# Three moves in the mixer of a hybrid block: which engine takes four w_ada tiles, where the expert bias rows are loaded, where silu(c) is computed

## Chip, cores and metric

The kernel runs on one core of a Trainium2 chip. The metric is the device time of one execution in microseconds (us); the median of several runs counts. Engine names as in the profile: PE is TensorE, DVE is VectorE, ACT is ScalarE, POOL is GpSimd, SP is SyncE, whose queue issues most loads from HBM.

## The reference, cut to what matters

One sequence of 256 tokens of width 1024, one conditioning vector `c`, all in float32.

```python
ada = (silu(c) @ w_ada + b_ada)                      # 6 x 1024 values
sh1, sc1, g1, sh2, sc2, g2 = split(ada, 6)
h = rmsnorm(x) * (1 + sc1) + sh1
xr, gr, q, k, v, gate_r, gate_a = split(h @ w_in + b_in)
y_rnn = rg_lru(conv(xr)) * gelu(gr)                  # RG-LRU: a scan over the tokens
y_att = sliding_window_attention(q, k, v, sinks)
merged = sigmoid(gate_r) * (y_rnn @ w_o_rnn) + sigmoid(gate_a) * (y_att @ w_o_attn)
x = x + g1 * rmsnorm(merged @ w_out)
h = rmsnorm(x) * (1 + sc2) + sh2
x = x + g2 * rmsnorm(moe(h))                         # top 4 of 32 experts: w1, b1, SwiGLU, w2, b2
```

The adaLN values `ada` are a matrix-vector product with 24 MB of w_ada. Only sh1 and sc1 are needed at the start; the rest is needed after the mixer.

## The kernel before, in words

**Memory.** All large weights come through one ring of 18 slots of 8 KB per partition (`ring`, L57), tag "w"; a load into a slot waits until the slot's last reader is done. The split parts hi and lo of a weight, and some intermediates, take slots of the same ring. Small intermediates of 2 KB per partition rotate through five buffers (`t2`, L72). PSUM is split into three banks with tag "p" and five with tag "a" (`bank`, L75). The order of the instructions on each engine is the program's order; nothing reorders them (L62).

**Start (L79 to L181).** SP loads c, x and the first w_ada and w_g1 tiles. ACT and DVE compute silu(c) spread over all partitions (`sc_`, L120, L121), then silu(c) as a column per chunk (`scc`: Sigmoid L124, product L125) and a column `one_each` (a reduction, L127); the last two are used only by the tiles of w_ada that PE takes. Then come the squares of x (ACT L131, DVE L132), the Sqrt and reciprocal (L158, L159), the normed rows `xn` (L161, L162) and their transposes. ACT has to load a function table before some functions; these loads are instructions of their own in the profile.

**The chunk loop (L234 to L274).** For each of the eight chunks k of the input width: DVE takes two dots with w_ada (L137), which give sh1 and sc1 of the chunk, two short operations make the factors `am` (L245, L247), ACT makes hT and its rounded part hTh (L253, L254), `split` (L184) makes the rounded part hi of the weights on ACT (L190) and the rest lo on DVE (L193), DVE makes hTl (L230). PE multiplies the chunk before into all eight banks (L267, then three passes of L273: hi with hTh, hi with hTl, lo with hTh).

**The mixer, steps 0 to 21 (L547, L620).** Step i issues loads (`ISSUE`, L35), splits the weights of step i+1 (ACT L190, DVE L193), runs the evacuation of step i-1 (`late_work`), and multiplies its own pair of weight tiles into a "p" bank (`mm_pair`, L285, matmuls at L295; step 5 is the v projection, `mm_v`, whose evacuation is DVE's L319). Steps 0 to 13 read h, 14 to 17 the attention's output `ya`, 18 to 21 the scan's output `yr`. Between these, `run` (L579) does the small tasks that `PLAN` (L34) names by letter, one list in the middle of a step and one after it: attention (M, X, E, N, T, P), convolution, gates and scans (s, c, m, R, g, h, d, D, q, S, y) and the later w_ada tiles (A). T is the transposes of the attention's products (PE L504), which need the products of N (DVE L492). y3, after step 17, makes the last quarter of yr (ACT L430, DVE L431).

**The later w_ada tiles.** Sixteen tiles remain, taken in the order of the letter A; index 4 and 5 stand after step 5 ("X02 E00 D0 A M10 A"), 9 after step 12, 10 after step 13, 11 in the middle of step 15. A tile whose index is in `ON_PE` (L37) goes to PE; the others are two dots on DVE (`ada_dot`, L136, L137). On PE a tile is eight matmuls into a "p" bank (`ada_mm`, L140, L145) with a copy by ACT (L148), and, at the next call of `run`, two matmuls and a copy (`ada_sum`, L151 to L155); the bank is held until then. How a tile is laid out in HBM follows `ON_PE`, on the host.

**After step 21 (L631 to L880).** ACT issues six loads, two halves of b2 (`b2s`, L649, 64 KB each) and four pieces of b1 (`b1t`, L654, 128 KB each, two `t2` buffers). DVE does some short operations (L631 to L662). ACT copies b1t into the rounded `b1r` (L664, twice), DVE takes the rest (L665, twice). Then steps 22 to 25 split the w_o tiles, evacuate the last step (`merge_r`, L607: DVE L612 and L613, ACT L614, DVE L615), and PE multiplies by w_out (L202) and spreads column vectors over the partitions (`spread`, L637, PE L643, ACT L644). Router and experts follow; SP loads the expert weights w1 and w2 (383 tiles of 1 MB) through the ring. The first of them are issued from step 21 on (letter e in `ISSUE`). SP and ACT put their loads on separate queues, but a load can also be made to wait for the landing of an earlier one, of either queue.

Of the kernel before, what the change touches and what calls it, by code (L numbers as in the profile page):

```python
# [8 lines left out]
F32 = mybir.dt.float32  # L9
F32R = mybir.dt.float32r  # L10
I32 = mybir.dt.int32
AF = mybir.ActivationFunctionType
OP = mybir.AluOpType
AX = mybir.AxisListType
ENG = mybir.EngineType

P = 128
# [4 lines left out]
E = 32  # L22
# [11 lines left out]
PLAN = {0: ('', 'g0 s1'), 1: ('', 'h0 c1 s0 c0'), 2: ('A', 'g1 m1 A'), 3: ('R1 A M00 m0', 'h1 A R0 X00'), 4: ('d1 M01', 's3 X01'), 5: ('d0 M02', 'X02 E00 D0 A M10 A'), 6: ('', 'M11 N00 X10 M12'), 7: ('E01 s2 X11 N01', 'X12 T000 A'), 8: ('P00 T010', 'E10 c2 A T011'), 9: ('P01 m2', 'N10 c3 E11'), 10: ('', 'N11 D1 g3 q0 q1 S0 T100'), 11: ('P10 A T110', 'R2 T111 g2 m3'), 12: ('R3 P11', 'h2 A'), 13: ('S1', 'h3 d2 D2 d3 D3 A'), 14: ('', 'q2 S2 q3 y0 S3'), 15: ('A y2', ''), 16: ('y1', 'A'), 17: ('', 'A y3'), 19: ('', 'A A')}  # L34
ISSUE = {-1: 'wwaww', 0: 'aw', 2: 'w', 5: 'a', 8: 'aw', 11: 'w', 14: 'aa', 19: 'aw', 21: 'w', 22: 'aw', 28: 'w', 29: 'w', 31: 'w', 33: 'a', 36: 'aa', 37: 'aw', 42: 'w', 43: 'wawwa', 49: 'w', 50: 'w', 52: 'awa', 54: 'w', 60: 'w', 64: 'e', 69: 'ww', 71: 'e', 72: 'e', 74: 'e', 76: 'eee'}  # L35
BIG = 3.0e38
ON_PE = (2, 4, 5, 7, 9, 11)  # L37

VEC = {}
_o = 0  # L40
# [11 lines left out]
def tile_hybrid_block(ctx: ExitStack, tc: tile.TileContext, x_in, c, vecs, rows, w_ada, w_g1, w_qk, w_v, w_gate,  # L52
                      w_bd, w_or, w_oa, w_o, w_router, w1, b1, w2, b2, out):
    nc = tc.nc
    consts = ctx.enter_context(tc.tile_pool(name="consts", bufs=1))
# [16 lines left out]
    def t2(shape=(512,), parts=P, name="t2"):  # L72
        return tmp.tile([parts] + list(shape), F32, name=name, tag="t2")
# [17 lines left out]
    def v(name, j=None):  # L91
        o, w = VEC[name]
        return vec[:, o:o + w] if j is None else vec[:, o + j:o + j + 1]
# [7 lines left out]
    b = bank("p")  # L101
# [19 lines left out]
    nc.vector.tensor_tensor(sc_, cb, sc_, op=OP.mult)  # L121
    nc.scalar.activation(warm, eps, AF.Sqrt)
    scc = consts.tile([P, KC], F32, name="scc")
    nc.scalar.activation(scc, v("c"), AF.Sigmoid)  # L124
    nc.vector.tensor_tensor(scc, v("c"), scc, op=OP.mult)  # L125
    one_each = consts.tile([P, 1], F32, name="one_each")
    nc.vector.tensor_reduce(one_each, ident.rearrange("p (a b) -> p a b", a=4)[:, :, 0], axis=AX.X, op=OP.add)  # L127
    lt = consts.tile([P, 4, 8], F32, name="lt")
    ada = consts.tile([P, 48], F32, name="ada")
    junk = rtile((2, D), "junk")  # L130
# [45 lines left out]
    o_, _ = VEC["b_ada"]  # L176
# [57 lines left out]
    for k in range(KC + 1):  # L234
# [6 lines left out]
        if k < KC:  # L241
            wt = rtile((2048,), "w")
            for h in range(2):
                nc.sync.dma_start(out=wt[:, h * D:(h + 1) * D], in_=w_g1[k, :, h * D:(h + 1) * D])
            nc.vector.scalar_tensor_tensor(am[:, 0, k:k + 1], ada[:, 8 + k:9 + k], scb[:, k:k + 1], v("n_pre_mix", k),  # L245
                                           op0=OP.add, op1=OP.mult)
            nc.vector.tensor_tensor(am[:, 1, k:k + 1], ada[:, k:k + 1], vec[:, o_ + k:o_ + k + 1], op=OP.add)  # L247
            if k == 1:
                lru_scales()
            hT[k] = t2((S,), name="hT")  # L250

            def make_h(k=k):
                nc.scalar.activation(hT[k], xnT[:, k], AF.Identity, scale=am[:, 0, k:k + 1], bias=am[:, 1, k:k + 1])  # L253
                nc.scalar.activation(hTh[:, k], hT[k], AF.Copy)  # L254

            if k < PLAIN:
                make_h()
                whl[k] = wt
            else:
                whl[k] = split(wt, make_h)  # L260
                low_h(k)
# [358 lines left out]
    for i in range(22):  # L620
        if i == 14:
            mg = big.tile([P, KC, S], F32, name="mg", tag="h")
        mid, after = PLAN.get(i, ("", ""))
        step(i, evac[i], lambda: run(mid))
        if i == 0:
            for f in range(8):
                b_ = g1b[4 + f // 2][:, (f % 2) * S:(f % 2 + 1) * S]
                nc.scalar.activation(gr[:, f], b_, AF.Identity, bias=v("b_gr", f))
        run(after)
# [14 lines left out]
            nc.scalar.activation(dst(i), b, AF.Copy)  # L644

    rws = big.tile([P, 2, D], F32, name="rws", tag="h")
    b2s = [big.tile([E, 512], F32, name="b2s", tag=tag) for tag in ("k", "v")]
    for i in range(2):
        nc.scalar.dma_start(out=b2s[i], in_=b2[:, i * 512:(i + 1) * 512])  # L649

    b1t, b1r = [t2() for _ in range(2)], consts.tile([P, 2, 512], F32R, name="b1r")
    for h in range(2):
        for i in range(2):
            nc.scalar.dma_start(out=b1t[h][64 * i:64 * i + 64], in_=b1[64 * h:64 * h + 64])  # L654
    sel = consts.tile([P, 64], F32R, name="sel")
    nc.vector.tensor_tensor(sel, ident[:, 0:64], ident[:, 64:128], op=OP.add)
    sel2 = consts.tile([64, E], F32R, name="sel2")
# [737 lines left out]
```

## Time and profile before

| | |
|---|---|
| median of 3 runs | 1255.26 us (1253.52 to 1258.53) |
| the profiled execution | 1256.51 us |
| its span, first to last instruction | 1254.9 us |
| mean granted PE clock | 0.969 |
| PE busy | 1156.5 us, 92% of the span |
| DVE busy | 479.5 us, 38% |
| ACT busy | 279.5 us, 22% |
| moved from HBM | 466.61 MB, 373 GB/s over the span |

Times in the rows are those of the profiled execution, from the start of its span. Busy shares are averages over stages with different limits: the mixer ends near 250 us, the router near 300, and the experts take the rest. What a part of the kernel is worth is read from the stage that it lies in. Granted clock 1.00 is 2.4 GHz, 0.50 is 1.2 GHz.

### The profile page before, as it was taken

The page shows a single profiled execution, that of the slowest core. Times are in us where ns is not written, and L with a number is a line of the kernel's source. Part 1 is how long each engine was busy: PE and PEld are TensorE (multiplying, and loading weights), DVE is VectorE, ACT ScalarE, POOL GpSimd, SP SyncE. Part 2 cuts the span into 40 slices and gives each one's busy share as a digit, 9 for nine tenths or more (in the row PEclk, how much of TensorE's full clock was granted, in tenths as well). Part 3 has the DMA queues.
Part 4 walks back from the last instruction along what each step waited for, and adds up shares of the span by engine and source line. Part 5 has one row for each costly group of instructions (what it writes and reads, how often), then busy time and mean ns, then how long its engine had stood idle before and what let it go on. Part 6 is the DMA issues. An engine that isn't in the chain of part 4 may idle for free. (4 is left out here: it accounts for less than half of the span.)

```text
span 1254.9 us, 15487 instructions
## 1 busy us (share of the span) xinstructions
PE 1156.5 (92%) x6003; PEld 558.9 (45%) x6003; DVE 479.5 (38%) x918; ACT 279.5 (22%) x523; POOL 10.4 (1%) x23
## 2 busy tenths in 40 slices
PE   7997999969899999999999999999979999998886
PEld 5995979946233333333343333333323333332322
DVE  6877787934522323222313223222223232222222
ACT  6466597233211101000101010000101110000002
POOL 0000000000100000000000000000000000000000
PEclk8998999979899999999999999999989999999999
DMA  9964456597889999999999999999999999999995
GB/s 366 405 248 168 168 202 272 232 343 294 363 334 422 421 421 421 421 421 421 421 420 421 422 394 420 421 421 421 421 418 420 420 421 420 421 421 421 421 420 213
DMA packets 68176, 468.74 MB, mean 374 GB/s; under 512 B 7616, under 2 KB 8000, under 8 KB 13696
## 3 DMA queue, kind: packets, MB, share of 16 engines
q1 hardware_dynamic: 67392, 466.67, 90.8%
q10 hardware_dynamic: 704, 1.02, 0.3%
q8 instruction: 48, 0.79, 0.3%
q14 instruction: 32, 0.26, 0.1%
HBM read 466.61 MB, written 1.05 MB: 373 GB/s over the span
## 5 line engine op out<-in xcount | busy, mean ns | idle before, releaser
L1008 PE MATMUL bank_a<-w,xg 128*64 128x512 f32 x2048 | 471.3, 605 | 11.4 <-PEq L1170 6.6
L1008 PEld LDWEIGHTS bank_a<-w,xg 128*64 128x64 f32 x2048 | 139.9, 139 | 293.6 <-issue 261.6
L1041 PE MATMUL bank_a<-w,aT 128*64 128x512 f32 x960 | 216.8, 600 | 9.1 <-ACT aT L1035 7.4
L1089 DVE TENSOR_SCALAR G<-bank_p,slot 128x256 fp32r<-128x256 f32 x32 | 15.5, 484 | 409.9 <-PE bank_p L1084 409.9
L1035 ACT ACTIVATE aT<-bank_p 128x512 f32<-128x512 f32 x31 | 18.5, 597 | 525.1 <-PE bank_p L1031 525.1
L1041 PEld LDWEIGHTS bank_a<-w,aT 128*64 128x64 f32 x960 | 66.1, 137 | 141.8 <-issue 115.7
L1062 DVE TENSOR_TENSOR ff<-ff,bank_p 128x512 f32<-128x512 f32 x124 | 79.7, 684 | 65.4 <-PE bank_p L1059 65.4
L193 DVE TENSOR_TENSOR lo<-w,hi 128x1024 fp32r<-128x1024 f32 x66 | 78.3, 1220 | 26.9 <-ACT hi L190 26.9
L1049 DVE SCALAR_TENSOR_TENSOR ys<-bank_a,gslot,ys 128x512 fp32r<-128x512 f32 x31 | 23.3, 751 | 146.6 <-ACT ys L1048 146.6
L190 ACT ACTIVATE hi<-w 128x1024 fp32r<-128x1024 f32 x66 | 66.1, 1052 | 6.1 <-DVE lo L193 4.2
L1059 PE MATMUL bank_p<-ys,G 64*128 64x512 f32 x248 | 49.2, 469 | 14.3 <-DVE ys L1049 13.5
L1048 ACT ACTIVATE ys<-bank_a,gslot 128x512 fp32r<-128x512 f32 x31 | 21.3, 688 | 167.6 <-PE bank_a L1041 164.0
L822 PE MATMUL bank_p<-pm,hth 128*128 128x256 f32 x112 | 33.3, 326 | 13.5 <-DVE pm L804 13.5
L137 DVE SCALAR_TENSOR_TENSOR w<-w,cs 128x1024 f32<-128x1024 f32 x36 | 42.5, 1220 | 0.0
L1059 PEld LDWEIGHTS bank_p<-ys,G 64*128 64x128 f32 x248 | 20.1, 196 | 47.5 <-issue 24.7
L295 PE MATMUL bank_p<-hTh,hi 128*128 128x256 f32 x208 | 31.5, 295 | 9.3 <-DVE vv L319 9.3
L822 PEld LDWEIGHTS bank_p<-pm,hth 128*128 128x128 f32 x112 | 22.6, 202 | 35.8 <-issue 18.3
L1004 PE MATMUL bank_a<-b1r,pick 128*128 128x512 f32 x124 | 37.7, 423 | 0.0
L1021 ACT ACTIVATE ys<-gl 128x512 f32<-128x512 f32 x33 | 20.8, 630 | 73.5 <-DVE gl L1020 73.5
L1004 PEld LDWEIGHTS bank_a<-b1r,pick 128*128 128x128 f32 x124 | 20.7, 188 | 29.4 <-issue 26.8
L295 PEld LDWEIGHTS bank_p<-hTh,hi 128*128 128x128 f32 x208 | 27.3, 195 | 13.2 <-DVE vv L319 9.8
L1020 DVE TENSOR_SCALAR gl<-bank_a 128x512 f32<-128x512 f32 x33 | 22.7, 686 | 22.3 <-PE bank_a L1008 16.9
(347 smaller groups left out, 1151.1 us busy)
## 6 DMA issues: line engine op xcount, KB each, us to landing
w<-in_w_dram SPq DMA_DIRECT2D x383, 1024.0 KB, 19.8
w<-in_w_ada_dram SPq DMA_DIRECT2D x16, 1024.0 KB, 6.5
w<-in_w_ada_dram SPq DMA_DIRECT2D x16, 512.0 KB, 10.2
w<-in_w_g_dram SPq DMA_DIRECT2D x16, 512.0 KB, 9.9
w<-in_w_gate_dram SPq DMA_DIRECT2D x8, 1024.0 KB, 5.3
w<-in_w_qk_dram SPq DMA_DIRECT2D x5, 1024.0 KB, 9.4
w<-in_w_oa_dram SPq DMA_DIRECT2D x4, 1024.0 KB, 6.3
w<-in_w_or_dram SPq DMA_DIRECT2D x4, 1024.0 KB, 8.2
```

Of the source, the lines that this page charges most:

```text
L137: nc.vector.scalar_tensor_tensor(wt[:, n], wt[:, n], 1.0, sc_, op0=OP.mult, op1=OP.mult, accum_out=ada[:, j:j + 1])
L190: nc.scalar.activation(hi[:, c_], w[:, c_], AF.Copy)
L193: nc.vector.tensor_tensor(lo[:, c_], w[:, c_], hi[:, c_], op=OP.subtract)
L295: nc.tensor.matmul(b[:, n], w[n][m][:, k * P:(k + 1) * P], z[l][:, k], start=k == 0 and i == 0 and (n == 0 or not late), stop=k == KC - 1 ...
L822: nc.tensor.matmul(ps[:, n], z[:, t, f * P:(f + 1) * P], pms[:, t].rearrange("p a b -> p (a b)"), start=t == 0 and n == 0 if len(ts) == 1 ...
L1004: nc.tensor.matmul(o, m.rearrange("p a b -> p (a b)"), z, start=False, stop=False)
L1008: nc.tensor.matmul(o[q * CAP:(q + 1) * CAP], xk(k), w1t[k][:, c0:c0 + 512], start=k == 0, stop=k == KC - 1)
L1020: nc.vector.tensor_scalar(gl, bb[0], LIMIT, None, op0=OP.min)
L1041: nc.tensor.matmul(y[q * CAP:(q + 1) * CAP], aT[:, k % 4, k // 4 * CAP:(k // 4 + 1) * CAP], w2t[k // 2][:, k % 2, q * 512:(q + 1) * 512], ...
L1049: nc.vector.scalar_tensor_tensor(lo, y, G[1], hi, op0=OP.mult, op1=OP.subtract)
L1059: nc.tensor.matmul(b[q], G[0][qs, t * P:(t + 1) * P], ys[i][qs], start=i == 1, stop=i == 0)
L1062: nc.vector.tensor_tensor(d, d, b[q], op=OP.add)
```

## The change

There are three edits. The list `ON_PE` has four indices instead of six: 4, 9 and 11 go from PE to DVE, and 10 goes from DVE to PE, so that no two of the listed ones are neighbours in the order. The six loads of b2 and b1 are issued inside the loop over the steps, by ACT, after step 17 and ahead of the tasks that follow it (a w_ada tile and y3), instead of after step 21; their readers stay where they were. The column silu(c) for PE and `one_each` are computed in the third chunk of the chunk loop (k = 2), after the two short operations for `am`, instead of at the start.

```diff
--- before.py
+++ after.py
@@ -34,7 +34,7 @@
 BIG = 3.0e38
-ON_PE = (2, 4, 5, 7, 9, 11)
+ON_PE = (2, 5, 7, 10)
 
 VEC = {}
 _o = 0
@@ -121,10 +121,7 @@
     nc.vector.tensor_tensor(sc_, cb, sc_, op=OP.mult)
     nc.scalar.activation(warm, eps, AF.Sqrt)
     scc = consts.tile([P, KC], F32, name="scc")
-    nc.scalar.activation(scc, v("c"), AF.Sigmoid)
-    nc.vector.tensor_tensor(scc, v("c"), scc, op=OP.mult)
     one_each = consts.tile([P, 1], F32, name="one_each")
-    nc.vector.tensor_reduce(one_each, ident.rearrange("p (a b) -> p a b", a=4)[:, :, 0], axis=AX.X, op=OP.add)
     lt = consts.tile([P, 4, 8], F32, name="lt")
     ada = consts.tile([P, 48], F32, name="ada")
     junk = rtile((2, D), "junk")
@@ -247,6 +244,10 @@
             nc.vector.tensor_tensor(am[:, 1, k:k + 1], ada[:, k:k + 1], vec[:, o_ + k:o_ + k + 1], op=OP.add)
             if k == 1:
                 lru_scales()
+            if k == 2:
+                nc.scalar.activation(scc, v("c"), AF.Sigmoid)
+                nc.vector.tensor_tensor(scc, v("c"), scc, op=OP.mult)
+                nc.vector.tensor_reduce(one_each, ident.rearrange("p (a b) -> p a b", a=4)[:, :, 0], axis=AX.X, op=OP.add)
             hT[k] = t2((S,), name="hT")
 
             def make_h(k=k):
@@ -622,6 +623,15 @@
             mg = big.tile([P, KC, S], F32, name="mg", tag="h")
         mid, after = PLAN.get(i, ("", ""))
         step(i, evac[i], lambda: run(mid))
+        if i == 17:
+            b2s = [big.tile([E, 512], F32, name="b2s", tag=tag) for tag in ("k", "v")]
+            for h in range(2):
+                nc.scalar.dma_start(out=b2s[h], in_=b2[:, h * 512:(h + 1) * 512])
+
+            b1t, b1r = [t2() for _ in range(2)], consts.tile([P, 2, 512], F32R, name="b1r")
+            for h in range(2):
+                for n in range(2):
+                    nc.scalar.dma_start(out=b1t[h][64 * n:64 * n + 64], in_=b1[64 * h:64 * h + 64])
         if i == 0:
             for f in range(8):
                 b_ = g1b[4 + f // 2][:, (f % 2) * S:(f % 2 + 1) * S]
@@ -644,14 +654,6 @@
             nc.scalar.activation(dst(i), b, AF.Copy)
 
     rws = big.tile([P, 2, D], F32, name="rws", tag="h")
-    b2s = [big.tile([E, 512], F32, name="b2s", tag=tag) for tag in ("k", "v")]
-    for i in range(2):
-        nc.scalar.dma_start(out=b2s[i], in_=b2[:, i * 512:(i + 1) * 512])
-
-    b1t, b1r = [t2() for _ in range(2)], consts.tile([P, 2, 512], F32R, name="b1r")
-    for h in range(2):
-        for i in range(2):
-            nc.scalar.dma_start(out=b1t[h][64 * i:64 * i + 64], in_=b1[64 * h:64 * h + 64])
     sel = consts.tile([P, 64], F32R, name="sel")
     nc.vector.tensor_tensor(sel, ident[:, 0:64], ident[:, 64:128], op=OP.add)
     sel2 = consts.tile([64, E], F32R, name="sel2")
```

## Rows read from the trace of the kernel before

**Rows 1.** The chain that ended last (page), shares of the span by engine.

```profile
DMA 22%; PE 3%; DVE 1%; issue 0%; ACT 0%; DVEq 0%; SPq 0%
```

**Rows 2.** By stage: length, busy PE PEld DVE ACT POOL, PEclk, DMA, GB/s.

```profile
142.00:180.00 38.00, 37.74 (x295) 31.14 (x293) 30.53 (x54) 30.90 (x71) 0.00 (x0) 1.00 0.48 177
213.60:247.60 34.00, 33.62 (x279) 33.30 (x278) 32.28 (x44) 12.58 (x15) 0.47 (x4) 1.00 0.73 290
122.38:140.77 18.39, 15.37 (x112) 14.77 (x113) 15.51 (x32) 8.48 (x25) 0.00 (x0) 0.81 0.31 115
260.00:270.00 10.00, 3.03 (x9) 2.56 (x10) 5.38 (x9) 4.03 (x6) 0.00 (x0) 0.50 1.02 409
400.00:1218.00 818.00, 770.42 (x3533) 279.42 (x3531) 215.93 (x398) 77.98 (x140) 0.00 (x0) 0.98 1.01 420
```

**Rows 3.** Timeline, start and last chunk: start, duration, engine, line, operation, tiles, [idle].

```profile
8.10 1.28 ACT L124 ACT_TABLE_LOAD   x1
11.10 1.28 ACT L158 ACT_TABLE_LOAD   x1 [0.45 <-DVE junk L132]
12.39 0.29 ACT L158 ACTIVATE rs<-small 128x2 f32<-128x2 f32 x1
9.79 1.22 DVE L132 SCALAR_TENSOR_TENSOR junk<-x 128x1024 f32<-128x1024 f32 x1
62.11 0.42 DVE L230 TENSOR_TENSOR hTl<-hT,hTh 128x256 fp32r<-128x256 f32 x1
64.96 0.88 PE L273 MATMUL bank_p<-hTl,hi 128*128 128x256 f32 x6
```

**Rows 4.** Timeline, TensorE at step 6, VectorE and TensorE at the transposes.

```profile
125.40 2.08 PE L295 MATMUL bank_p<-hTh,hi 128*128 128x256 f32 x8 [9.31 <-DVE vv L319]
138.87 1.90 DVE L492 TENSOR_TENSOR att<-att,den 128x512 f32<-128x512 f32 x3
141.73 1.03 PE L504 MATMUL bank_a<-ident,att 128*128 128x128 f32 x8
```

**Rows 5.** Timeline, one w_ada tile on each engine: L145 and one of two L137.

```profile
190.78 1.07 PE L145 MATMUL bank_p<-w,scc 128*32 128x256 f32 x16
202.86 1.22 DVE L137 SCALAR_TENSOR_TENSOR w<-w,cs 128x1024 f32<-128x1024 f32 x1
```

**Rows 6.** Waits of SP, 190 to 380 us; timeline, 250 to 276 us.

```profile
SPq L66 <- DMA b2s<-in_b_dram: 12.8, 1, 12.8
SPq L66 <- DMA t<-in_b_dram: 8.3, 4, 3.2
...
250.06 0.63 ACT L614 ACTIVATE mgp<-mg 128x512 fp32r<-128x512 f32 x1 [2.80 <-DVE mg L613]
250.92 2.46 ACTq L654 DMA_DIRECT2D t<-in_b_dram  x4
262.35 0.63 ACT L664 ACTIVATE b1r<-t 128x512 fp32r<-128x512 f32 x1 [5.20 <-DMA t<-in_b_dram]
...
252.21 0.16 DVE L662 TENSOR_TENSOR slot<-slot 128x1 f32<-128x1 f32 x1
...
251.84 0.62 PE L202 MATMUL bank_a<-hi,mgp 128*128 128x512 f32 x2
266.97 1.11 PE L643 MATMUL bank_p<-ident,ada 128*128 128x128 f32 x4 [11.22 <-DVE t L612]
267.74 0.77 PE L202 MATMUL bank_a<-hi,mgp 128*128 128x512 f32 x1
275.41 0.39 PE L202 MATMUL bank_a<-hi,mgp 128*128 128x512 f32 x1
```

**Rows 7.** Load issued 213.6 to 214.2 us; timeline of steps 17, 18.

```profile
w<-in_w_ada_dram SPq DMA_DIRECT2D x1, 1024.0 KB, 7.8
...
225.21 2.01 ACT L190 ACTIVATE hi<-w 128x1024 fp32r<-128x1024 f32 x2 [4.20 <-DVE lo L193]
...
227.98 0.69 DVE L431 TENSOR_TENSOR yr<-gr,yr 128x512 fp32r<-128x512 f32 x1
```

## Prediction, made before the change was run

> **What bounds the kernel now.** Read the chain that ended last first [rows 1]: 22% of the span is transfers of expert weights and everything else together is some 5%, so the end is set by a stream of loads. The table by stage confirms it [rows 2]: from 400 to 1218 us the DMA share is 1.01 at 420 GB/s, and the change touches nothing there. A transfer-bound tail moves only as a whole, by as much as the work ahead of it hands over sooner; that work ends before 400 us, and each microsecond saved in it counts once. So each part is priced in its own stage. In the same table, from 142 to 180 us TensorE is busy 37.74 of 38 us; from 213.6 to 247.6 us TensorE is busy 33.62 and VectorE 32.28 of 34 us, both nearly full; from 260 to 270 us TensorE works 3.03 of 10 us at a granted clock of 0.50. That last hole is the dearest, and the waits around it lead straight to one part of the change [rows 6].
>
> **silu(c) moved.** The program starts with a table load for L124's Sigmoid at 8.10 us and one for L158's Sqrt at 11.10 us, 1.28 us each; behind the second, L158 runs at 12.39 [rows 3]. The Sigmoid stands between two Sqrt, so without it both loads go. The DVE square L132, held to 9.79 us by the two silu operations ahead of it, can start at about 8.1, when ScalarE's first load would have begun: 1.69 sooner. With the load of 1.28 that is 2.97 us, which TensorE inherits through xn. Will it keep them? In the chunk loop VectorE is as busy as TensorE: its last hTl is ready at 62.11 + 0.42 = 62.53 us, and TensorE's pass over it starts at 64.96 [rows 3]. If VectorE gained nothing and the two moved short operations cost it 0.3 us (0.16 us each, as L662 [rows 6]), TensorE could still move by 64.96 − 62.85 = 2.1 us. Bounds 2.1 and 3.0; VectorE's first dots start earlier too, so I take **2.8**. The Sigmoid's load in the third chunk falls where ScalarE waits for VectorE: nothing there. The Trainium skill (ScalarE: Activation LUTs, What ACT_TABLE_LOAD costs) charges a drain of some 1.4 us beside a load of 1.28. By that the two loads would give 2.8 us more, 5.6; the row, whose Sqrt starts at 12.39 = 11.10 + 1.28 + 0.01, shows no drain behind the load, so the sum goes without it.
>
> **The tile of step 5 (index 4).** Today two tiles in a row after step 5 run on TensorE, and each holds one of three p banks; the third holds the v projection. Step 6 then waits 9.31 us, until 125.40, for the DVE evacuation of v (L319) [rows 4]. With index 4 on VectorE a bank is free, and step 6 can start some 9 us sooner. That is not the gain: the transposes L504 at 141.73 need att_norm's products (L492), which end at 138.87 + 1.90 = 140.77, and VectorE has to do two more dots of 1.22 us ahead of them [rows 4, 5]. From 122.38 to 140.77 VectorE is busy 15.51 of 18.39 us [rows 2]: 2.9 us of waits, on ScalarE and TensorE work that now comes sooner. If all go, L492 ends at 140.77 + 2.44 − 2.9 = 140.3 and TensorE gains 1.4 us; if none go, it loses 140.77 + 2.44 − 141.73 = 1.5. Most of the waits are for engines that gain, so I take **1.0**. From 142 us TensorE is the bound and carries it on.
>
> **Indices 9, 10 and 11.** Two tiles go from TensorE to VectorE and one comes back. TensorE is relieved of one tile net, 1.07 us of L145; VectorE gets one net, 2 × 1.22 = 2.44 [rows 5]. Bounds: +1.07 if TensorE is the limit throughout, −2.44 if VectorE is. TensorE is the fuller one (33.62 against 32.28 [rows 2]), and index 10's dots leave ScalarE-bound time: I take **0.6**. Here a rule speaks against the change: the Trainium skill (Perfetto Trace Analysis, Identifying the Most-Contended Engine) holds that occupancy is a fair measure of nearness to the limit for Vector, but not for Tensor matmuls, which are pipelined. By it VectorE at 32.28 of 34 would be the limit, and this part would come out at −2.44; no row settles it, so it is a rival below.
>
> **The b rows.** ScalarE issues six loads behind the copy L614 of 250.06 (the last four of them take 2.46 us); then ScalarE waits for their landing at both copies L664, 5.20 us before the second [rows 6]. Queued behind these copies are the split of the next w_o tile and DVE's L665, lo and L612, and TensorE's second spread (L643) waits 11.22 us, to 266.97, for L612's bank. SP suffers as well: its weight loads wait 12.8 us for the landing of b2s and 8.3 us in four waits for b1's, so the expert stream stands still before 252 [rows 6]. Loaded at step 17, the rows lie there. The copy L614 ends at 250.69, so L664 runs at 250.7 and 251.3 where the second now runs at 262.35: 11.05 us sooner. VectorE's short operations up to 252.37 (L662), which now lie in the wait, stay ahead of L665; this takes back about 1.0. So TensorE resumes near 256.9, 10.0 us sooner. Then the clock, granted at 0.50 in this stretch [rows 2]: the first matmul of L202 after the hole takes 0.77 us, the last one of the 24 takes 0.39, and between their starts lie 275.41 − 267.74 = 7.67 us. Before the hole two take 0.62, one 0.39, so one follows another by 0.23, and 23 steps by 5.3: the hole costs 2.4 us more by what it does to the clock, and only 1.2 us of it stay. Bounds 10.0 (the clock gives nothing) and 13.6 (11.22 + 2.4); I take **12.4**.
>
> **What the loads cost at step 17.** Six issues at 2.46/4 us are 3.7 us of ScalarE. As the SP waits show, a load here is held by the landing of an earlier one, so ScalarE may also stand until the w_ada load in flight, issued near 213.7 and landing 7.8 us later, is in: 221.5 [rows 7]. Behind it stand y3's copy L430 and the split for step 19. Their readers on VectorE come at 227.98 (L431) and after, and ScalarE's next split waits 4.20 us for VectorE anyway [rows 7]: about 6 us of cover. The 0.64 MB delay the w_o loads by some 1.5 us at 420 GB/s; ScalarE splits these long after. Cost 0; without the cover the first microseconds over 227.98 would count in full.
>
> **Sum.** 2.8 + 1.0 + 0.6 + 12.4 = 16.8 us. The profiled execution took 1256.51 us (1254.9 of span and 1.6 around it), which makes 1239.7; it stood 1.25 above the median of 1255.26, so against the median I forecast **1238.5**. By the bounds, 2.1 − 1.5 − 2.4 + 10.0 = 8.2 gives 1247.1, and 3.0 + 1.4 + 1.1 + 13.6 = 19.1 gives 1236.2, both against the median.
>
> **Rivals.** *VectorE is the limit of the whole mixer.* Net two tiles more on it cost 4.9 us and step 6 gives nothing: 12.4 + 2.8 − 4.9 = 10.3, so 1245.0. For it: 32.28 of 34 us. Against: 30.53 of 38 between 142 and 180 [rows 2], and the waits from 122 to 141. *The stream does not start sooner.* The weight loads also need free ring slots; if those come free only near 250, the transfer side gains 2 us of the b part, and with 4.4 of the others it comes to 6.4: 1248.9. For it: other waits of SP than those for b rows exist. Against: the first experts' loads are released by the work that moves. *Slower.* At step 17 ScalarE is held in its issues by landings, y3 is late, and TensorE stands before its yr matmuls. This decides only if ScalarE resumes after 227.98 + 16.8 = 244.8; released at 250, and with 2.4 us of a low clock, the kernel would take 1255.3 + 5.2 + 2.4 = 1262.9. Against it: 7.8 us for a load in that stretch.
>
> **How the numbers follow.** Forecast 0.66; VectorE the limit 0.15; stream not sooner 0.14; slower 0.05. A measurement of this kernel tells 0.5%, 6.3 us, from no change: faster is below 1249.0. The third case lies on that line and is halved: faster 0.66 + 0.15 + 0.07 = 0.88, same 0.07, slower 0.05. The range runs from the good end, 1236.2, less the 3 us by which single runs of this kernel stand off their median, 1233, to the stream's case, 1249.
>
> **What would show it.** Right: no wait at L664, TensorE's hole before the second spread under 2 us and L202 there at 0.39; no SP wait for b rows; xn and the first g1 matmuls about 3 us sooner; no 9 us wait ahead of step 6, L504 some 3.8 us earlier (2.8 + 1.0). Wrong: a wait of TensorE for yr or lo between 215 and 245; a new wait of ScalarE at step 17 beyond 228; a share of expert weights in the chain that begins no sooner than now.

## The result, and the profile after

The changed kernel takes 1235.97 us (median of 4 runs, 1233.44 to 1238.33), the kernel before 1255.49 in the same comparison: a ratio of 0.984, 95% interval 0.981 to 0.987. That is 19.5 us less; the forecast was 1238.5, 16.8 less, with a range from 1233 to 1249. The profiled execution of the changed kernel was the slowest of its four, 1238.33 us.

The page of the changed kernel, its span and the chain that ended last, answers to [rows 1]:

```profile
span 1236.7 us, 15408 instructions
...
PE 16%; DMA 8%; DVE 1%; ACT 1%; issue 0%; DVEq 0%; SPq 0%
```

The expert weights' transfers are still in the chain, but with 8% instead of 22%: in this execution a long run of matmuls of the experts, each behind the one before, takes their place. Which of the two ends last there differs among the profiled executions (with the late copies, below, it is 19% transfers and 6% matmuls), and in the table by stage (columns as in [rows 2]) the tail is as full as before:

```profile
128.00:132.00 4.00, 4.00 (x22) 3.35 (x22) 3.97 (x8) 0.00 (x0) 0.00 (x0) 0.66 0.00 0
136.00:174.00 38.00, 37.46 (x293) 30.83 (x290) 32.46 (x57) 31.20 (x72) 0.00 (x0) 1.00 0.50 181
205.50:239.60 34.10, 32.73 (x271) 32.33 (x270) 32.38 (x46) 9.71 (x11) 0.47 (x4) 1.00 0.85 313
255.00:260.00 5.00, 3.72 (x18) 2.32 (x16) 2.81 (x3) 3.07 (x5) 0.00 (x0) 1.00 0.86 333
260.00:265.00 5.00, 4.96 (x15) 3.96 (x16) 0.75 (x2) 0.69 (x2) 0.00 (x0) 0.66 1.02 426
380.00:1198.00 818.00, 770.61 (x3539) 279.22 (x3537) 215.94 (x398) 77.97 (x140) 0.00 (x0) 0.99 1.01 420
```

From 380 to 1198 us the DMA share is 1.01 at 420 GB/s, as from 400 to 1218 before: the tail has the same length and begins sooner. To see where the 19 us come from, five instructions of TensorE serve as marks, read from the timelines: the first matmul of step 0, the first transpose L504 of the second group (T010, in the middle of step 8), the last matmul of step 21, the second spread (the second group of four L643 matmuls, 266.97 in [rows 6]), and the first matmul of the first expert (L1008). The four stretches between them, and the rest up to the end of the span, are:

| kernel | step 0 at | to T010 | to the last matmul | to the 2nd spread | to the 1st expert | to the end |
|---|---|---|---|---|---|---|
| before | 68.80 | 77.78 | 101.07 | 19.33 | 39.39 | 948.50 |
| changed | 65.92 | 74.34 | 99.33 | 9.28 | 37.93 | 949.87 |
| difference | −2.88 | −3.44 | −1.74 | −10.05 | −1.46 | +1.37 |

Each column is the place of one part of the change: the start, index 4, indices 9 to 11, the b rows, and the clock behind them. These are single executions, and kernels that are alike in a stretch still scatter there, as the table of experiments shows: by 2 us at the start, up to T010 and up to the first expert, by 4 us in the rest. Up to the first expert 19.56 us are gained; in this execution 1.37 of them are lost behind it, which leaves the 18.2 between the two spans.

(Lines of the changed kernel are shifted: up to L167 by 3 less than before, L504 is L505, L202 L199, L643 L653, L664 L666, L1008 L1010.)

The timeline of the start and the last chunk, to be laid beside [rows 3]:

```profile
7.00 1.28 ACT L122 ACT_TABLE_LOAD   x1
9.82 0.30 ACT L155 ACTIVATE rs<-small 128x2 f32<-128x2 f32 x1 [0.28 <-DVE junk L129]
8.48 1.23 DVE L129 SCALAR_TENSOR_TENSOR junk<-x 128x1024 f32<-128x1024 f32 x1 [0.24 <-DMA x<-in_x_dram]
61.48 0.42 DVE L227 TENSOR_TENSOR hTl<-hT,hTh 128x256 fp32r<-128x256 f32 x1
62.08 0.88 PE L274 MATMUL bank_p<-hTl,hi 128*128 128x256 f32 x6
```

Between the Sigmoid of L120 and the squares only one table load is left, that of L122's Sqrt, and L155's Sqrt (L158 before) runs at 9.82 with none right ahead of it. Seen from the load of L122 (6.59 before, 7.00 now) it gained 2.98 us. VectorE's last hTl is ready only 0.63 us sooner, and TensorE's pass over it starts at 62.08 with 0.18 us to spare behind 61.90: the cover was used up nearly to the end, as worked out.

Step 6 and the transposes, beside [rows 4]:

```profile
112.14 1.22 PE L296 MATMUL bank_p<-hTh,hi 128*128 128x256 f32 x8
118.31 0.61 PE L151 MATMUL bank_p<-one_each,w 128*128 128x1 f32 x4 [3.04 <-ACT w L145]
126.97 1.75 PE L447 MATMUL bank_a<-kT,qT 64*128 64x256 f32 x6 [3.59 <-DVE att L466]
135.42 1.04 PE L505 MATMUL bank_a<-ident,att 128*128 128x128 f32 x8
134.52 1.89 DVE L493 TENSOR_TENSOR att<-att,den 128x512 f32<-128x512 f32 x3
```

The wait of 9.31 us before step 6 is gone. Two others have come, of 3.04 us for ScalarE's copy of the one tile left and of 3.59 us for an a bank that VectorE's mask step X10 still reads.

Steps 17 and 18, and the stretch of the b rows, beside [rows 6, 7]:

```profile
203.49 0.81 ACTq L629 DMA_DIRECT2D b2s<-in_b_dram  x2
204.90 1.90 ACTq L634 DMA_DIRECT2D t<-in_b_dram  x3
211.40 2.01 ACT L187 ACTIVATE hi<-w 128x1024 fp32r<-128x1024 f32 x2 [3.92 <-DVE lo L190]
216.05 0.39 PE L296 MATMUL bank_p<-yr,lo 128*128 128x256 f32 x1 [0.85 <-DVE lo L190]
217.19 0.39 PE L296 MATMUL bank_p<-yr,lo 128*128 128x256 f32 x1 [0.52 <-DVE lo L190]
242.56 1.14 ACT L666 ACTIVATE b1r<-t 128x512 fp32r<-128x512 f32 x2
...
248.87 0.65 PE L653 MATMUL bank_p<-ident,ada 128*128 128x128 f32 x4 [1.16 <-DVE t L613]
249.28 0.48 PE L199 MATMUL bank_a<-hi,mgp 128*128 128x512 f32 x1
254.60 0.39 PE L199 MATMUL bank_a<-hi,mgp 128*128 128x512 f32 x1
258.90 0.50 PE L199 MATMUL bank_a<-lo,mgp 128*128 128x512 f32 x1 [0.76 <-DVE lo L190]
```

The loads are issued between 203.49 and 206.80, without a wait for a landing, and no load of SP waits for the b rows any more. TensorE waits 0.85 and 0.52 us for lo at 216 and 217 us, which the prediction had named as a sign of being wrong; what these two waits are worth is weighed below, with the tiles. The two copies (now L666) run without a wait at 242.56, and TensorE's hole before the second spread is 1.16 us instead of 11.22. The next w_out's 24 matmuls take 5.32 us from the first start to the last, not 7.67. In the row by stage the clock falls once more, though, to a mean of 0.66 from 260 to 265 us, behind three short waits of TensorE (0.39, 0.76 and 0.18 us) such as that at 258.90. The same three waits stand in the kernel before, and there the clock stayed at 1.00:

```profile
279.71 0.50 PE L202 MATMUL bank_a<-lo,mgp 128*128 128x512 f32 x1 [0.76 <-DVE lo L193]
...
275.00:280.00 5.00, 3.85 (x20) 2.76 (x19) 1.57 (x2) 3.07 (x5) 0.00 (x0) 1.00 0.96 341
280.00:290.00 10.00, 9.83 (x45) 7.74 (x45) 5.54 (x12) 4.67 (x14) 0.00 (x0) 1.00 0.72 257
```

### The profile page after: what moved, and what is told of

Its sections match the earlier page's. It is cut to its first block, busy times and chain, and to the rows that moved or that the text cites. A ratio compares the mean times of both kernels' runs of the same rounds, so it can differ in the third digit from the quotient of the medians.

```text
span 1236.7 us, 15408 instructions
## 1 busy us (share of the span) xinstructions
PE 1151.7 (93%) x5963; PEld 555.9 (45%) x5963; DVE 483.7 (39%) x926; ACT 275.7 (22%) x517; POOL 10.4 (1%) x23
## 5 line engine op out<-in xcount | busy, mean ns | idle before, releaser
L1010 PE MATMUL bank_a<-w,xg 128*64 128x512 f32 x2048 | 470.2, 604 | 11.6 <-DVEq L1172 6.5
L1010 PEld LDWEIGHTS bank_a<-w,xg 128*64 128x64 f32 x2048 | 139.4, 138 | 292.4 <-issue 259.5
L134 DVE SCALAR_TENSOR_TENSOR w<-w,cs 128x1024 f32<-128x1024 f32 x40 | 47.3, 1220 | 1.8 <-DMA w<-in_w_ada_dram 1.7
L1061 PEld LDWEIGHTS bank_p<-ys,G 64*128 64x128 f32 x248 | 19.5, 191 | 48.1 <-issue 25.0
L1022 DVE TENSOR_SCALAR gl<-bank_a 128x512 f32<-128x512 f32 x33 | 22.7, 686 | 22.6 <-PE bank_a L1010 17.1
L824 PE MATMUL bank_p<-pm,htl 128*128 128x256 f32 x112 | 30.5, 299 | 0.0
```

What stands on the lines that cost most here:

```text
L134: nc.vector.scalar_tensor_tensor(wt[:, n], wt[:, n], 1.0, sc_, op0=OP.mult, op1=OP.mult, accum_out=ada[:, j:j + 1])
L824: nc.tensor.matmul(ps[:, n], z[:, t, f * P:(f + 1) * P], pms[:, t].rearrange("p a b -> p (a b)"), start=t == 0 and n == 0 if len(ts) == 1 ...
L1010: nc.tensor.matmul(o[q * CAP:(q + 1) * CAP], xk(k), w1t[k][:, c0:c0 + 512], start=k == 0, stop=k == KC - 1)
L1022: nc.vector.tensor_scalar(gl, bb[0], LIMIT, None, op0=OP.min)
L1061: nc.tensor.matmul(b[q], G[0][qs, t * P:(t + 1) * P], ys[i][qs], start=i == 1, stop=i == 0)
```

## The experiments

Each kernel below is the changed one with a single edit, unless it says more. Its stretches, in the columns of the table above, with the median and the ratio to the kernel before (95% interval):

| kernel | step 0 at | to T010 | to last | to spread | to expert | to end | median, ratio |
|---|---|---|---|---|---|---|---|
| b rows after step 21 | 65.32 | 73.86 | 99.32 | 18.94 | 38.32 | 947.76 | 1246.4, 0.993 (0.991 to 0.995) |
| old list of tiles | 65.45 | 77.55 | 101.07 | 9.27 | 36.44 | 947.82 | 1241.0, 0.989 (0.987 to 0.991) |
| silu(c) at the start | 68.92 | 75.87 | 99.31 | 9.27 | 37.73 | 947.91 | 1237.7, 0.986 (0.984 to 0.987) |
| 9, 11 on TensorE, not 10 | 67.25 | 73.87 | 101.07 | 9.26 | 37.92 | 947.39 | 1237.2, 0.985 (0.983 to 0.987) |
| 13 on TensorE too | 66.08 | 75.72 | 101.05 | 7.76 | 36.63 | 947.77 | 1235.5, 0.983 (0.981 to 0.985) |
| b rows after 21, late copies | 65.82 | 73.88 | 99.35 | 10.01 | 37.96 | 947.63 | 1235.7, 0.984 (0.981 to 0.986) |
| both Sigmoid together | 65.62 | 74.34 | 99.33 | 9.26 | 37.90 | 949.84 | 1236.4, 0.985 (0.983 to 0.986) |
| index 4 in an a bank | 66.30 | 72.47 | 99.34 | 9.27 | 38.31 | 948.23 | 1235.3, 0.983 (0.980 to 0.986) |
| spread at 24 | 66.29 | 75.73 | 99.33 | 9.26 | 34.19 | 951.08 | 1233.8, 0.981 (0.979 to 0.984) |
| a bank, spread at 24 | 65.10 | 72.47 | 99.35 | 9.25 | 36.15 | 950.41 | 1234.4, 0.983 (0.982 to 0.985) |
| M12 moved, spread at 24 | 66.25 | 73.89 | 99.32 | 9.27 | 34.19 | 948.16 | 1234.0, 0.984 (0.982 to 0.985) |
| all three | 65.15 | 72.48 | 99.33 | 9.29 | 36.05 | 949.32 | 1234.0, 0.983 (0.981 to 0.985) |

**The three parts undone, one at a time.** First the b rows:

```diff
-        if i == 17:
-            b2s = [big.tile([E, 512], F32, name="b2s", tag=tag) for tag in ("k", "v")]
...
     rws = big.tile([P, 2, D], F32, name="rws", tag="h")
+    b2s = [big.tile([E, 512], F32, name="b2s", tag=tag) for tag in ("k", "v")]
...
```

> The changed kernel with the six loads of b2 and b1 put back after step 21; the other two edits stay. Theory (ScalarE's wait for the landing at L664 holds the split, L612 and TensorE's second spread, and the hole lowers the clock): up to step 21 nothing moves (last matmul of the mixer near 239.6 us), the second spread comes some 10 us later than 248.9 and the first expert's first matmul 11.5 us later than 286.8, near 298.3; median near 1247.5. Rival (the three edits overlap, the b rows are hidden once the other parts come sooner): first expert below 291, median below 1240.

ScalarE's wait at the second copy and TensorE's second spread in this kernel's timeline:

```profile
252.82 0.63 ACT L665 ACTIVATE b1r<-t 128x512 fp32r<-128x512 f32 x1 [5.31 <-DMA t<-in_b_dram]
257.44 1.11 PE L644 MATMUL bank_p<-ident,ada 128*128 128x128 f32 x4 [10.82 <-DVE t L613]
```

Only the last columns move. The hole is back, 10.82 us, the second spread lies 9.66 us further from the last matmul, and the median is 1246.4, 10.4 us more (ratio 0.993 against 0.984). The theory holds, but the first expert comes at 295.76 and not at 298.3: the stretch up to it is only 0.39 us longer than in the changed kernel. That 99.32 us from T010 to the last matmul are the 99.33 of the changed kernel also shows that the six issues at step 17 cost nothing there.

Then the list of tiles:

```diff
-ON_PE = (2, 5, 7, 10)
+ON_PE = (2, 4, 5, 7, 9, 11)
```

> The changed kernel with the old list of six tiles on TensorE (2, 4, 5, 7, 9, 11). Theory (two tiles in a row hold two of three p banks, and that costs 3.4 us until the first transposes L505; the indices 9 to 11 cost another 1.7): L505 near 138.9 instead of 135.4, first expert's first matmul near 292.0 instead of 286.8, median near 1241. Rival (VectorE limits the mixer, so giving it two tiles more net gained nothing): first expert at 286.8 or sooner, median 1236 or lower.

The two columns of the mixer return to 77.55 and 101.07, against 77.78 and 101.07 before; the median rises by 5.0 us. The rival, for which VectorE is the limit, falls. (The first transposes came at 138.16.)

And silu(c):

```diff
+    nc.scalar.activation(scc, v("c"), AF.Sigmoid)
+    nc.vector.tensor_tensor(scc, v("c"), scc, op=OP.mult)
...
-            if k == 2:
-                nc.scalar.activation(scc, v("c"), AF.Sigmoid)
...
```

> The changed kernel with scc and one_each computed at the start again. Theory (two table loads of 1.28 us and the two VectorE operations stand before xn; TensorE carries the shift through the chunk loop and the mixer): step 0 starts at 68.8 instead of 65.9 and the first expert's first matmul comes 2.9 us later, near 289.7; median near 1239. Rival (VectorE, which gained only 0.6 us in the chunk loop, or a later wait takes the gain away): first expert within 1 us of 286.8, median within 1 us of 1236.

Step 0 starts at 68.92, 3.0 us later; the median is 1.7 above the changed kernel's, below the 1239 that was expected and with intervals that overlap. The marks decide here, not the medians. The three losses, 10.4, 5.0 and 1.7, make 17.1 of the 19.5 by the medians. In their own columns the parts undone alone are worth 10.05 (9.66 and 0.39), 4.95 and 3.00 us, against 11.51, 5.18 and 2.88 in the table of the change; what differs most is the stretch up to the first expert, 0.39 against 1.46.

**Which of the tiles.** Only index 4 moved:

```diff
-ON_PE = (2, 5, 7, 10)
+ON_PE = (2, 5, 7, 9, 11)
```

> The changed kernel with the list (2, 5, 7, 9, 11): index 4 alone stays with VectorE, 9 and 11 are back on TensorE and 10 back on VectorE. Theory (near 200 us the exchange of 9, 10, 11 gains 1.7 us, since the tile on TensorE at index 10 frees VectorE and ScalarE where they limit): L505 stays at 135.4, first expert's first matmul 1.7 us later, near 288.5; median near 1237.7. Rival (VectorE is the limit from 205 us on, and one tile less on it helps): first expert up to 2.4 us sooner, near 284.4; median near 1233.6.

From T010 to the last matmul it takes 101.07 us, to the hundredth what it took before: all of the 1.74 us come from the exchange of 9, 10 and 11. VectorE has one tile less in this kernel and it is slower, so the rival falls. TensorE's timeline near 200 us, the tile at index 11 and its sums, and the waits beside it:

```profile
200.97 1.21 PE L296 MATMUL bank_p<-ya,lo 128*128 128x256 f32 x8 [0.51 <-DVE lo L190]
202.12 1.07 PE L142 MATMUL bank_p<-w,scc 128*32 128x256 f32 x16
206.09 0.50 PE L151 MATMUL bank_p<-one_each,w 128*128 128x1 f32 x4
206.86 2.17 PE L296 MATMUL bank_p<-ya,hi 128*128 128x256 f32 x16 [0.26 <-ACT ada L152]
209.40 1.22 PE L296 MATMUL bank_p<-ya,lo 128*128 128x256 f32 x8 [0.37 <-DVE lo L190]
```

One tile costs TensorE 1.07 + 0.50 us. Three waits of 0.51, 0.26 and 0.37 stand beside it; the changed kernel has two others instead, 0.85 and 0.52 us for lo. From T010 to the last matmul TensorE is busy 98.34 us here and 96.40 in the changed kernel, and idle 2.73 and 2.94: the gain is work that TensorE no longer does, and the waits take 0.2 of it back.

**One more tile on TensorE.**

```diff
-ON_PE = (2, 5, 7, 10)
+ON_PE = (2, 5, 7, 10, 13)
```

> The changed kernel with index 13 on TensorE as well (2, 5, 7, 10, 13). From 203 to 222 us VectorE is now busy 19.00 of 19 us and TensorE waits 0.85 and 0.52 us for lo. Theory (VectorE limits there, but by no more than these waits, and the tile costs TensorE 1.6 us): the last matmul of the mixer comes 104 to 104.5 us after the first transposes as in the changed kernel (104.2), median within 1 us of 1236. Rival (VectorE limits all the way to 240 us): 2.4 us sooner, near 101.8 us, median near 1233.6.

Neither came: the last matmul is 105.89 us after the first transposes, 1.7 later than in the changed kernel. The rows show a new wait, which neither theory had:

```profile
217.57 0.38 ACT L145 ACTIVATE w<-bank_p 128x256 f32<-128x256 f32 x1 [10.54 <-PE bank_p L142]
218.38 1.99 ACT L187 ACTIVATE hi<-w 128x1024 fp32r<-128x1024 f32 x2
...
219.42 0.47 PE L296 MATMUL bank_p<-yr,hi 128*128 128x256 f32 x2 [1.91 <-ACT hi L187]
```

ScalarE's copy of the tile stands ahead of y3 and of the split for step 19, waits 10.54 us for the matmuls that come after step 17, and TensorE then waits 1.91 us for that split. The second spread follows sooner (7.76 instead of 9.28), so up to there only 0.2 us are lost, and the median is the same. Whether VectorE is the limit just there, with ScalarE out of the way, this run leaves open.

**Whose wait it was.** In the kernel before, ScalarE waits at the copies and SP's weight loads stand behind the same landings. One edit separates them: the loads go back after step 21, and the copies go behind the loop over steps 22 to 25.

```diff
     rws = big.tile([P, 2, D], F32, name="rws", tag="h")
+    b2s = [big.tile([E, 512], F32, name="b2s", tag=tag) for tag in ("k", "v")]
...
-    for h in range(2):
-        nc.scalar.activation(b1r[:, h], b1t[h], AF.Copy)
-        nc.vector.tensor_tensor(b1r[64:, h], b1t[h][64:], b1r[64:, h], op=OP.subtract)
...
             spread(lambda i: rws[:, 1, halves(i)], a2)
             nc.scalar.activation(warm, eps, AF.Sqrt)
+    for h in range(2):
+        nc.scalar.activation(b1r[:, h], b1t[h], AF.Copy)
+        nc.vector.tensor_tensor(b1r[64:, h], b1t[h][64:], b1r[64:, h], op=OP.subtract)
```

> The changed kernel with the six b loads back after step 21, and the two copies into b1r (ScalarE, with VectorE's part) moved behind the loop over steps 22 to 25, so that nothing near step 22 waits for the landing; SP's loads of expert weights are still issued behind these six. Theory (the price of the old place was paid by what is queued behind ScalarE's wait at the copies, not by the held-up expert loads): second spread near 248 us, first expert's first matmul within 2 us of the changed kernel's 286.8, median within 2 us of 1236, though SP still waits some 12 us for b2s. Rival (the expert stream, started some 10 us later, sets the time): the first expert is hardly later, but the median stays above 1243.

SP's waits in this kernel, and ScalarE's split and TensorE's second spread in its timeline:

```profile
SPq L66 <- DMA b2s<-in_b_dram: 13.0, 2, 12.7
SPq L66 <- DMA t<-in_b_dram: 7.8, 4, 3.0
```

```profile
244.97 2.00 ACT L187 ACTIVATE hi<-w 128x1024 fp32r<-128x1024 f32 x2 [2.86 <-DMA t<-in_b_dram]
249.07 0.65 PE L644 MATMUL bank_p<-ident,ada 128*128 128x128 f32 x4 [1.90 <-DVE t L613]
```

SP waits as long as before the change, ScalarE 2.86 us where it waited 11, and next to nothing is lost: second spread at 249.07, first expert at 287.02 against 286.80, median 1235.7. The price of the old place was paid by what was queued behind ScalarE's copies; the held-up weight loads cost nothing that the marks or the median show.

**What the silu part bought.** Both Sigmoid together at the start, so that no table changes between them:

```diff
     nc.scalar.activation(sc_, cb, AF.Sigmoid)
+    nc.scalar.activation(scc, v("c"), AF.Sigmoid)
     nc.vector.tensor_tensor(sc_, cb, sc_, op=OP.mult)
     nc.scalar.activation(warm, eps, AF.Sqrt)
+    nc.vector.tensor_tensor(scc, v("c"), scc, op=OP.mult)
...
```

> The changed kernel with scc and one_each back at the start, but with their Sigmoid right behind the other Sigmoid (L120), ahead of the Sqrt warm-up; the product and the reduction on VectorE stand after it. Theory (the price of the old start was the two table loads, which a Sigmoid between two Sqrt brings): no table load but the two that the changed kernel has up to L170's Exp; from the landing of c to the first transposes of xn within 0.5 us of the changed kernel, not 2.6 us more; median within 1 us of 1236. Rival (the work on VectorE ahead of L132, or the wait for the vectors' landing, was the price): 1.5 us or more of the 2.9 come back; median 1237.5 or more.

ScalarE's timeline at the start:

```profile
6.71 0.19 ACT L122 ACTIVATE scc<-vec 128x8 f32<-128x8 f32 x1
6.92 1.28 ACT L124 ACT_TABLE_LOAD   x1
8.21 0.20 ACT L124 ACTIVATE small<-small 128x1 f32<-128x1 f32 x1
9.64 0.29 ACT L158 ACTIVATE rs<-small 128x2 f32<-128x2 f32 x1 [0.19 <-DVE junk L132]
```

The second Sigmoid takes 0.19 us and the one load left stands behind it, with the Sqrt right after (6.92 + 1.28 + 0.01). From the Sigmoid of L120, which waits for c, to the first transpose of xn it takes 5.62 us, as in the changed kernel, against 8.61 before; step 0 starts at 65.62, the median is 1236.4. The two operations on VectorE still stand ahead of the squares, so it was the table loads. Moving the work into the third chunk is one way to be rid of them, and no better than this.

**The p bank or the pair.** Index 4 back on TensorE, with its sum in an a bank:

```diff
-ON_PE = (2, 5, 7, 10)
+ON_PE = (2, 4, 5, 7, 10)
-    def ada_mm(wt):
+    def ada_mm(wt, tag="p"):
-        b = bank("p")
+        b = bank(tag)
-            sums_due.append((*ada_mm(w), 2 * j))
+            sums_due.append((*ada_mm(w, "a" if j == order_a[4] else "p"), 2 * j))
```

> The changed kernel with index 4 back on TensorE, in one of the five a banks instead of one of the three p banks: two tiles in a row again, and no third p bank taken. Theory (what cost 9 us of TensorE at step 6 was the p bank, and what limits the first transposes now is VectorE, which loses 2.4 us of dots): no wait of some 9 us before step 6, and L505 1 to 2.4 us sooner after the start of step 0 than the 69.5 us of the changed kernel; median 1233.5 to 1235. Rival (two tiles in a row are the trouble by themselves, or the a banks run short for the attention products): L505 2 us or more later after step 0, median 1238 or above.

TensorE's timeline, the second tile and step 6:

```profile
112.52 1.07 PE L142 MATMUL bank_p<-w,scc 128*32 128x256 f32 x16
113.52 1.22 PE L296 MATMUL bank_p<-hTh,hi 128*128 128x256 f32 x8
```

Step 6 starts at once behind the second tile, so the trouble was the third p bank and not the pair. The first transposes come 67.48 us after step 0, and T010 72.47: 1.4 us better than the best of the kernels with index 4 on VectorE (73.86). The median, 1235.3, does not tell them apart from the changed kernel.

**TensorE's gaps behind the spread.**

```diff
-        if i == 23:
+        if i == 24:
             spread(lambda i: rws[:, 1, halves(i)], a2)
             nc.scalar.activation(warm, eps, AF.Sqrt)
```

> The changed kernel with the spread of a2 (and the Sqrt warm-up behind it) one step later, at 24 instead of 23, so that ScalarE's split of the last w_o tile does not stand behind copies that wait for TensorE. Theory (the gaps of TensorE at 257 to 260 us, 1.3 us, come from that order, and the low clock at 260 to 264, some 1.6 us, follows from them): from the second spread to the first expert's first matmul 35 to 36.6 us instead of 37.9; median 1233 to 1234.7. Rival (the residual's chain on ScalarE and VectorE sets that stretch, TensorE's gaps are slack): 37.5 to 38.5 us, median unchanged.

The table by stage of this kernel, in the same columns:

```profile
255.00:260.00 5.00, 5.00 (x27) 4.20 (x26) 4.46 (x4) 3.70 (x6) 0.00 (x0) 1.00 0.91 339
260.00:265.00 5.00, 5.00 (x24) 4.13 (x23) 1.84 (x5) 1.67 (x5) 0.00 (x0) 1.00 1.02 433
265.00:270.00 5.00, 5.00 (x26) 4.01 (x25) 4.12 (x10) 3.92 (x12) 0.00 (x0) 1.00 0.97 374
```

TensorE is busy 15.00 of 15 us at a clock of 1.00, where the changed kernel has the gaps and then 0.66. The stretch to the first expert takes 34.19 us, 3.7 less, more than was expected. Not all of it is the spread's: two kernels with the spread at 23 take 36.44 and 36.63 us (old list of tiles; 13 on TensorE too), because the clock stays at 1.00 there behind the same three waits. Against these the move is worth 2.25 and 2.44 us. The median is 1233.75, ratio 0.981 (0.979 to 0.984), an interval that overlaps the changed kernel's. T010 was late in this execution (75.73) and the experts long (951.08), so the profiled span shows only 0.8 of it.

**Together.** Index 4 in an a bank and the spread at 24 in one kernel; the spread at 24 with the score product M12 moved; and all three. The move of M12 is:

```diff
-6: ('', 'M11 N00 X10 M12'), 7: ('E01 s2 X11 N01', 'X12 T000 A')
+6: ('', 'M11 N00 X10'), 7: ('M12 E01 s2 X11 N01', 'X12 T000 A')
```

> The changed kernel with both variants that looked better: index 4 on TensorE in an a bank, and the spread of a2 at step 24. Theory (1.4 us from the dots that leave VectorE ahead of the second half of the first transposes, and 2 to 3.7 us from TensorE's gaps and the low clock behind them): first expert's first matmul 3.4 to 5 us sooner than 286.8, at 282 to 283.5; median near 1232. Rival (a gain in the mixer is used up by a longer wait behind it, as the two variants alone moved the median by only 0.7 and 2.2): no sooner than 284.8, median 1233.5 to 1236.

> The changed kernel with the spread of a2 at step 24, and with attention's third score product (M12) moved from after step 6 into the middle of step 7, so that TensorE does not stand before step 7 for an a bank that VectorE's X10 holds. Theory (the gain of step 6, 3.4 us in the changed kernel and 1.9 to 3.9 in the others, varies with where the low clock behind this wait falls; without the wait VectorE alone sets it): step 8 is always reached 3.9 us sooner than before the change, counted from step 0; first expert near 283; median near 1232.5. Rival (the wait only moves, to the middle of step 7, and with it the low clock): 1.9 to 3.4 us, median 1234 or above.

> The changed kernel with index 4 on TensorE in an a bank, M12 in the middle of step 7, and the spread of a2 at step 24. Theory (the three act on different waits and add up as far as the low clock does not return): step 8 reached 5.3 us sooner than before the change, counted from step 0; from the second spread to the first expert 34.2 us, or 36.2 if the clock falls there; first expert near 281 to 283; median 1231.5 to 1234. Rival (what is handed over sooner is used up in the first experts): first expert near 281 to 283, but the median at 1235 or above.

The marks come as expected: the first expert at 282.32, 282.91 and 282.30, T010 after 72.47, 73.89 and 72.48 us, which is what VectorE allows with and without the dots of index 4: TensorE waits 0.89, 2.12 and 1.15 us for L493 ahead of the second half of the first transposes. In the first and the third the clock falls to a mean of 0.66 from 245 to 250 us, and their stretch to the first expert is 36 us, not 34.2. But the medians, 1234.4, 1234.0 and 1234.0, are 1.6 to 2 us below the changed kernel's and not the 3.7 to 4.2 by which the first expert is sooner, counted from step 0; the medians forecast for them are missed, the last one barely, and the first lies where its rival had it. All intervals overlap with that of the changed kernel, 0.981 to 0.987: these versions hand over earlier, and that they are faster in the end isn't shown.

## Why the prediction was right, and where its terms were off

**The bound** was read rightly: the tail kept its length, and what the stages before it gained came out at the end.

**The b rows**, 12.4 forecast, 11.5 measured: 10.05 from the last matmul to the second spread, as the sum had it (10.0), and 1.46 for the clock instead of 2.4. The term that was mis-sized is the clock. The low clock of the hole did go (5.32 instead of 7.67 us for the 24 matmuls), but in this execution it came back at 260 to 265 us, behind three short waits that did nothing to it in the kernel before. In kernels with the same instructions there it fell at that place (both Sigmoid together, index 4 in an a bank), or already behind the wait of some 1.1 us at the second spread (silu(c) at the start; 9, 11 on TensorE, not 10), or not at all: 36.44 and 36.63 us with the old list of tiles and with 13 on TensorE, 2.95 and 2.76 less than before the change. So this stretch gives between 1.1 and 2.95 us, and which of these an execution gets, the change does not decide; what does stays open. The sentence that SP suffers as well was true and worth nothing, as the kernel with late copies shows; the rival in which the stream starts no sooner falls with it.

**Index 4**, 1.0 forecast with an upper bound of 1.4, 3.44 measured. The step that failed is that L504 needs all of att_norm's products, ending at 138.87 + 1.90, a microsecond ahead of its start. It needs the first of the three: `att_turn` reads the tile that `att_norm` makes first. So VectorE did not hold L504 in the kernel before. TensorE worked without a gap from step 6 at 125.40 up to it:

```profile
140.77 1.12 PE L295 MATMUL bank_p<-hTh,lo 128*128 128x256 f32 x8
```

Its own queue, late by the 9.31 us wait and at a mean clock of 0.70 up to 132 us, set the 141.73, and there was more to gain than 1.4 us before VectorE would set it. In the kernel with the late copies the first group of L504 is seen in two halves:

```profile
133.78 0.60 PE L505 MATMUL bank_a<-ident,att 128*128 128x128 f32 x4
135.27 0.63 PE L505 MATMUL bank_a<-ident,att 128*128 128x128 f32 x4 [0.89 <-DVE att L493]
```

The second half starts 0.84 us behind the start of L493 (134.43 there), when the first product is done. With that, the prediction's own numbers would have put it at 138.87 + 2.44 − 2.9 + 0.84 = 139.25, against 142.16 for the second half before the change: 2.9 us. Another 1.0 is VectorE's: it reached L493 4.35 us sooner (134.52 against 138.87), 2.88 of them from the start, so 1.47 where the waits counted gave 0.5; another wait, of 0.79 us, lay just ahead of the window that was read. That makes the 3.9 that VectorE allows; the changed kernel's execution stayed 0.5 below it, since TensorE's own queue was late again (no wait at 135.42). The best executions gain 3.9 (73.86 to 73.88 in three of them), the worst 1.9 to 2.1 (75.7 to 75.9 in three): the same instructions, with the low clock on other matmuls behind the new waits. In the row by stage it lies at 128 to 132 us in the changed kernel. And the move to VectorE was not needed for it: with the sum in an a bank the tile stays on TensorE and T010 comes 1.4 us sooner still.

**Indices 9, 10, 11**, 0.6 forecast, 1.74 measured, above the bound of 1.07. The bound counted a tile's L145 alone and left out its two sums (0.50 us of L154). TensorE's busy time in the stretch fell by 1.93 us (98.33 to 96.40), of which 1.07 + 0.50 are the tile's own; the rest, 0.36, is not resolved here. Its idle time did not fall (2.74 and 2.94). The sign was right: TensorE set this stretch, and the kernel with 9 and 11 back on TensorE, one tile less on VectorE and 1.74 us slower, shows it. VectorE is close behind, as the two waits for lo show. The Trainium skill's rule on occupancy (Perfetto Trace Analysis, Identifying the Most-Contended Engine) does not speak against this, though the prediction took it so: for Tensor the rule puts the busy share of the weight loads (and the floating-point work done) in place of the matmuls' busy share. In [rows 2] the weight loads (PEld) are busy 33.30 of 34 us, above VectorE's 32.28, and the run agrees. With two engines this full, the row alone could still not say which.

**silu(c)**, 2.8 forecast, 2.88 measured, and the price was the loads, as said. (The load at 8.10 is not the program's first, as the prediction calls it; those of L120 and L122, at 1.34 and 6.59, stand ahead of it and remain.) That the size fits so closely is in part luck: eleven kernels with the new start reach step 0 between 65.10 and 67.25 us, in part because c lands sooner or later (L120 starts between 5.44 and 6.39). Counted from the Sigmoid of L120 to the first transpose of xn it is 8.61 us before and 5.62 after, 2.99 less. A load's drain of some 1.4 us as the Trainium skill has it (ScalarE: Activation LUTs, What ACT_TABLE_LOAD costs) would have made it 5.6; neither the measured gain nor the row at 6.92 above shows it.

**Step 17**, nothing forecast, nothing measured: 99.33 us from T010 to the last matmul with the loads there, 99.32 without.

So the total, 16.8 against 19.5, is short by the two tile terms, 3.6 together, and over by 0.9 in the b rows; errors of opposite sign bring it nearer than its terms are. Of the rivals, none held. That of VectorE holds in places: it sets the first transposes after the change, and TensorE waits for its lo at 216 us.

## What to carry to other kernels

When loads are issued early but stand in front of a copy on the same in-order queue, ask what is queued behind the copy: moving either the loads or the copy cures it, and the held-up stream may cost nothing. Before you say that an operation waits for a group of instructions, look which of them it reads. When two engines are both nearly full, count everything that a piece of work makes each of them do, its small sums as well, rather than choose by busy share.

## What was not expected of the hardware

Waits of TensorE were followed by stretches at the lower of the two clocks: in the changed kernel means of 0.66 at 128 to 132 us, behind waits of 3.04 and 3.59 us, and at 260 to 265 us, behind waits of only 0.39, 0.76 and 0.18 us. Where these stretches fell, and whether they came at all, changed from one execution to the next with the same instructions and the same waits. The stretch from step 0 to T010 took 73.9, 74.3 or 75.7 to 75.9 us in kernels that are alike from step 0 to there, that from the second spread to the first expert 36.4 to 38.3, and the experts' part between 947.4 and 951.1 us. What a small edit is worth is better read from marks within the stage than from the end, and from more than one execution.
